# First feed-forward stage: norm weights applied where the transposes are emptied, a fixed order of the first conversions, constants loaded later

## The chip, the cores and the metric

One core of a Trainium2 chip runs the kernel in one launch. The metric is device time in microseconds, the median of several executions; the profile is one further execution, taken by the hardware profiler.

## What is computed

An encoder of two layers over 256 tokens of width 1024, in fp32. Each layer is a feed-forward block, an attention block (differential in the first layer, neighbourhood in the second) and a second feed-forward block, each with an RMS norm ahead of it and one behind:

```python
def _rmsnorm(x, g):
    y = xf * lax.rsqrt(jnp.mean(xf * xf, axis=-1, keepdims=True) + EPS)
    return (y * g.astype(jnp.float32)).astype(x.dtype)

def _swiglu(x, wg, wu, wd):
    return (jax.nn.silu(x @ wg) * (x @ wu)) @ wd

    h = h + FFN_RES * _rmsnorm(_swiglu(_rmsnorm(h, g[0]), ffn1_wg[i], ...), g[1])
```

The hidden width of the feed-forward blocks is 2816. The change is in the very first of them, up to the point where its pipeline is full.

## The kernel before

The 256 tokens are two tiles of 128 rows, `h[0]` and `h[1]`. Every matrix is kept as a sum of two fp32r parts, hi and lo, and a product is three: hi x hi, hi x lo, lo x hi. Weights come in pieces of 512 KB (128 x 1024 fp32). The class `Weights` plans them in one list. `load` issues a piece's DMA on SP's queue into one of four raw buffers; `split` makes hi on ScalarE (L130, a copy that rounds) and lo on VectorE (L131, raw minus hi), each in two halves of 512 columns, into one of nine part buffers. `get`, called where products need a piece, first splits that piece, then up to four ahead, then loads up to eight ahead. A raw buffer is free, and SP may issue the next DMA, when VectorE has made both lo halves.

The program is recorded in this order, and a scheduler sets the order on each engine by priorities (`high_priority` moves a block forward) and by `issue_after`, which puts instructions behind a given one on their engine. Every engine then runs its instructions in order, and waits are put in where data or buffers ask for them.

The first stage goes so. SP issues the two halves of `h[0]`, pieces 0 and 1 of `wg`, `h[1]`, pieces 2 and 3, two gain rows that are spread over 128 partitions (`gain`, L250), then the four pieces of `wu` (4 to 7), four column pieces (8 to 11) and so on. ScalarE issues one small DMA for the first gain row, and TensorE spreads it over the partitions with two matmuls against ones (L243) into two PSUM banks `g_first`. `first_norm` squares a tile on ScalarE (L282), takes the inverse root on POOL and multiplies by it and by the gain on VectorE (L307). `norm_T` transposes the two halves on TensorE, each into one PSUM bank (L365), and empties each bank with one 128x512 operation on ScalarE (hi, L355) and one on VectorE (lo, L356). POOL's queue loads `rope`, `mask` and `subg`, which are used in later stages.

`gu_rows` (through `proj_rows`, L380 to L383) makes four row products of 512 columns: g0 and g1 from `wg` for tiles 0 and 1, u0 and u1 from `wu`. Each has 24 matmuls: for each of eight blocks k of 128 rows hi x hi and hi x lo, and at the end lo x hi for all eight. `act` is the SiLU of g0 (L482), `gated` multiplies u0 by it on VectorE (L487) into `a`, which `to_T` transposes. From p = 2 on `gu_cols` makes products by columns (L414, L415): this is the column pass, and it uses the same pieces for both tiles. `down` (L438) adds products with `wd`.

Of the kernel before, what the change touches and what calls it, by code (L numbers as in the profile page):

```python
# [26 lines left out]
WARM = 1  # L27
# [49 lines left out]
class Weights:  # L77


    def __init__(self, tc, raw_pool, part_pool):  # L80
        self.tc = tc
        self.nc = tc.nc
        self.extras = []
        self.raw_pool = raw_pool
        self.part_pool = part_pool
        self.src = []
        self.key = {}
        self.raw = {}
        self.parts = {}
        self.n_dma = 0  # L90
        self.n_split = 0
        self.live = set()
        self.floor = 0

# [22 lines left out]
    def split(self, upto):  # L117
        nc = self.nc
        while self.n_split < min(upto, len(self.src)):
            i = self.n_split  # L120
            self.load(i + 1)
            ap = self.src[i]
            a, b = ap.shape[1], ap.shape[2]
            raw = self.raw.pop(i)
            hi = self.part_pool.tile([P, UE], F32R, tag="hi", name=f"whi{i}")
            lo = self.part_pool.tile([P, UE], F32R, tag="lo", name=f"wlo{i}")
            n = a * b
            for c in range(0, n, PIECE):
                e = slice(c, c + PIECE)
                nc.scalar.activation(hi[:, e], raw[:, e], AF.Copy)  # L130
                nc.vector.tensor_tensor(out=lo[:, e], in0=raw[:, e], in1=hi.bitcast(F32)[:, e], op=ALU.subtract)  # L131
            self.parts[i] = (
                hi[:, :n].rearrange("p (a b) -> p a b", b=b),
                lo[:, :n].rearrange("p (a b) -> p a b", b=b),
            )
            self.n_split += 1

    def get(self, key):
        i = self.key[key]
        self.split(i + 1)  # L140
        self.split(min(i + 1 + SPLIT_AHEAD, self.floor + PART_BUFS))
        self.load(min(i + 1 + DMA_AHEAD, self.n_split + RAW_BUFS))
        return self.parts[i]
# [8 lines left out]
def encoder_kernel(ctx, tc, x, norm_g, f1g, f1u, f1d, f2g, f2u, f2d,  # L152
# [79 lines left out]
    g_row = l4p.tile([1, D], F32, tag="l4", name="g_row")  # L232
    nc.scalar.dma_start(g_row, norm_g[0, 0:1, :])
    ones = t2p.tile([1, P], F32, tag="t2", name="ones")
    nc.vector.memset(ones, 1.0)
    warm = t2p.tile([P, NC], F32, tag="t2", name="warm")
    nc.vector.memset(warm, 0.0)
    for i in range(WARM):
        wps = ps_mm.tile([P, 512], F32, tag="mm", name=nm("warm_ps"))
        nc.tensor.matmul(wps, warm[:, :P], warm, start=True, stop=True)  # L240
# [7 lines left out]
    def gain(li, j, queue=nc.sync):  # L248
        t = gp.tile([P, D], F32, tag="gain", name=nm("gain"))
        queue.dma_start(t, bcast(norm_g[li, j, :], P))  # L250
        return t

# [4 lines left out]

    ident = const.tile([P, P], F32, name="ident")
# [3 lines left out]
    nc.vector.memset(mhalf, -0.5)  # L262
    rope = const.tile([P, NH, 2, 16], F32, name="rope")
    nc.gpsimd.dma_start(rope, ropec.rearrange("(t p) a b -> p t a b", p=P))
    mask = const.tile([P, GRID_W], F32, name="mask")
    nc.gpsimd.dma_start(mask, maskc)
    subg = const.tile([P, P], F32, name="subg")
    nc.gpsimd.dma_start(subg, bcast(dsub[0], P))
    bias = const.tile([P, 8, 6, GRID_W], F32, name="bias")

# [40 lines left out]
    def first_norm(t, gain_t):  # L311
        with tc.high_priority(offset=HP):
            return first_norm_(t, gain_t)

# [3 lines left out]

    def first_norm_(t, gain_t):
        ss = sm.tile([P, 2], F32, tag="ss2", name=nm("ss2"))  # L320
        for b, s in enumerate(HALVES):
            square(h[t][:, s], 1.0 / 32.0, ss[:, b:b + 1])
        return prenorm(t, gain_t, ss)
# [52 lines left out]
    def proj_rows(ps, xT, t, keys):  # L376
        parts = [W.get(key) for key in keys]
        w = [(wh[:, j, :], wl[:, j, :]) for wh, wl in parts for j in range(wh.shape[1])]
        for kt, (wh, wl) in enumerate(w):
            nc.tensor.matmul(ps, xT[0][:, t, kt, :], wh, start=kt == 0, stop=False)  # L380
            nc.tensor.matmul(ps, xT[0][:, t, kt, :], wl, start=False, stop=False)  # L381
        for kt, (wh, wl) in enumerate(w):
            nc.tensor.matmul(ps, xT[1][:, t, kt, :], wh, start=False, stop=kt == KT - 1)  # L383
# [87 lines left out]
    def ffn(key, li, gpre, xg1, xT, gpost, last, aside=None):  # L471
# [3 lines left out]
        def gu_rows(nme, t):  # L475
            ps = mm_tile()
            proj_rows(ps, xT, t, [(key, nme, 0, j) for j in range(KT * NC // UE)])
            return ps
# [41 lines left out]
        if key == "f10":  # L520
            s0 = act(gu_rows("g", 0))
            norm_T(xg1, xT, 1)
# [308 lines left out]
    xg0 = first_norm(0, g_first)  # L831
# [8 lines left out]
    xg1, xT = ffn("f10", 0, gain(0, 2), xg1, xT, gain(0, 1), False)  # L840
# [47 lines left out]
```

## Time and profile before

| | us |
|---|---|
| median of three runs | 1022.96 |
| lowest, highest | 1022.93, 1028.88 |
| profiled execution | 1023.75 |
| its span, first to last instruction | 1022.0 |

Times in the rows below are microseconds from the start of the span. A timeline row gives the start, the time until the last of its instructions ended, the engine, the line, what was written and read, how many instructions are taken together, and in brackets the engine's idle time before it and what ended that. PE is TensorE, ACT ScalarE, DVE VectorE. Matmuls overlap: their rate is read from start to start.

### The profile page before, as it was taken

The page shows a single profiled execution, that of the slowest core. Times are in us where ns is not written, and L with a number is a line of the kernel's source. Part 1 is how long each engine was busy: PE and PEld are TensorE (multiplying, and loading weights), DVE is VectorE, ACT ScalarE, POOL GpSimd, SP SyncE. Part 2 cuts the span into 40 slices and gives each one's busy share as a digit, 9 for nine tenths or more (in the row PEclk, how much of TensorE's full clock was granted, in tenths as well). Part 3 has the DMA queues.
Part 4 walks back from the last instruction along what each step waited for, and adds up shares of the span by engine and source line. Part 5 has one row for each costly group of instructions (what it writes and reads, how often), then busy time and mean ns, then how long its engine had stood idle before and what let it go on. Part 6 is the DMA issues. An engine that isn't in the chain of part 4 may idle for free.

```text
span 1022.0 us, 14666 instructions
## 1 busy us (share of the span) xinstructions
PE 1002.6 (98%) x5342; PEld 842.8 (82%) x5342; DVE 667.3 (65%) x1240; ACT 586.3 (57%) x1235; POOL 22.9 (2%) x38
## 2 busy tenths in 40 slices
PE   8999999999999999999999999999999999999997
PEld 5788888888777788888888888888898878888885
DVE  6766666577777666667577676657865477556572
ACT  6655556566776555656456555546765366555551
POOL 1000000000001000000000000000000010000000
PEclk9999999999999999999999999999999999999999
DMA  8866666375524666665377667646742446666631
GB/s 276 266 187 189 192 191 187 113 239 169 165 84 139 229 208 180 192 186 188 108 234 245 194 191 216 195 134 205 229 121 102 124 145 225 187 192 179 205 104 42
DMA packets 120825, 182.84 MB, mean 179 GB/s; under 512 B 5729, under 2 KB 87649, under 8 KB 120754
## 3 DMA queue, kind: packets, MB, share of 16 engines
q1 hardware_dynamic: 120608, 181.65, 57.3%
q8 instruction: 42, 0.69, 0.3%
q0 software_dynamic: 144, 0.26, 0.2%
q14 instruction: 29, 0.24, 0.1%
q10 hardware_dynamic: 2, 0.00, 0.0%
HBM read 180.84 MB, written 1.05 MB: 178 GB/s over the span
## 4 chain that ended last, share of the span: by engine, by line
PE 87%; DMA 4%; ACT 4%; DVE 3%; issue 1%; POOL 0%; SPq 0%; DVEq 0%; POOLq 0%; ACTq 0%
PE mm L414 25%; PE acc L438 24%; PE mm L415 13%; PE mm L380 5%; PE mm L381 5%; PE mm L383 5%; PE mm L438 2%; PE tr L365 2%; PE tr L702 2%; DMA raw<-in_ffn_wg_dram 2%; DVE wlo L131 2%; DMA raw<-in_ffn_wu_dram 1%; ACT whi L130 1%; DMA raw<-in_na_w_in_dram 1%; PE mm L397 1%
## 5 line engine op out<-in xcount | busy, mean ns | idle before, releaser
L131 DVE TENSOR_TENSOR wlo<-raw,whi 128x512 fp32r<-128x512 f32 x656 | 425.2, 686 | 178.5 <-ACT whi L130 170.8
L130 ACT ACTIVATE whi<-raw 128x512 fp32r<-128x512 f32 x656 | 379.2, 624 | 210.6 <-PE mm L414 52.8
L414 PE MATMUL mm<-xT,whi 128*128 128x512 f32 x1152 | 408.3, 399 | 0.8 <-DVE g L498 0.7
L415 PE MATMUL mm<-xT,wlo 128*128 128x256 f32 x1152 | 323.9, 281 | 0.0
L414 PEld LDWEIGHTS mm<-xT,whi 128*128 128x128 f32 x1152 | 216.7, 188 | 54.9 <-DVE g L498 1.7
L415 PEld LDWEIGHTS mm<-xT,wlo 128*128 128x128 f32 x1152 | 218.0, 189 | 1.1
L438 PE MATMUL acc<-whi,hT 128*128 128x512 f32 x704 | 197.3, 391 | 0.0
L438 PEld LDWEIGHTS acc<-whi,hT 128*128 128x128 f32 x704 | 130.3, 188 | 26.9
L380 PE MATMUL mm<-whi,xT 128*128 128x512 f32 x272 | 110.6, 407 | 2.9 <-ACT xT L355 2.8
L438 PE MATMUL acc<-wlo,hT 128*128 128x512 f32 x352 | 111.7, 391 | 0.0
L381 PE MATMUL mm<-wlo,xT 128*128 128x512 f32 x272 | 108.5, 399 | 0.0
L438 PEld LDWEIGHTS acc<-wlo,hT 128*128 128x128 f32 x352 | 66.1, 188 | 14.2
L383 PE MATMUL mm<-whi,xT 128*128 128x512 f32 x272 | 67.4, 390 | 0.0
L380 PEld LDWEIGHTS mm<-whi,xT 128*128 128x128 f32 x272 | 51.9, 191 | 16.4 <-ACT xT L355 5.2
L381 PEld LDWEIGHTS mm<-wlo,xT 128*128 128x128 f32 x272 | 51.9, 191 | 12.1 <-DVE wlo L131 2.0
L383 PEld LDWEIGHTS mm<-whi,xT 128*128 128x128 f32 x272 | 51.1, 188 | 10.5
L498 DVE TENSOR_TENSOR u<-mm,u 128x256 f32<-128x256 f32 x72 | 30.3, 421 | 32.1 <-ACT u L497 32.0
L497 ACT ACTIVATE g<-mm 128x256 f32<-128x256 f32 x72 | 26.9, 374 | 36.3 <-PE mm L415 36.3
L355 ACT ACTIVATE hT<-a 128x512 fp32r<-128x512 f32 x36 | 22.7, 630 | 41.1 <-DVE a L487 41.1
L498 DVE TENSOR_TENSOR g<-mm,g 128x256 f32<-128x256 f32 x72 | 30.2, 420 | 14.2 <-ACT g L497 14.2
L497 ACT ACTIVATE u<-mm 128x256 f32<-128x256 f32 x72 | 26.9, 374 | 17.0 <-PE mm L415 17.0
L356 DVE TENSOR_TENSOR hT<-a,hT 128x512 fp32r<-128x512 f32 x36 | 24.9, 693 | 17.3 <-ACT hT L355 16.1
(113 smaller groups left out, 811.0 us busy)
## 6 DMA issues: line engine op xcount, KB each, us to landing
raw<-in_ffn_wg_dram SPq DMA_DIRECT2D x88, 512.0 KB, 4.6
raw<-in_ffn_wu_dram SPq DMA_DIRECT2D x88, 512.0 KB, 4.5
raw<-in_ffn_wd_dram SPq DMA_DIRECT2D x88, 512.0 KB, 4.3
raw<-in_diff_w_in_dram SPq DMA_DIRECT2D x24, 512.0 KB, 4.8
raw<-in_na_w_in_dram SPq DMA_DIRECT2D x24, 512.0 KB, 4.8
gain<-in_norm_g_dram SPq DMA_DIRECT2D x11, 512.0 KB, 5.3
raw<-in_diff_w_out_dram SPq DMA_DIRECT2D x8, 512.0 KB, 3.9
raw<-in_na_w_out_dram SPq DMA_DIRECT2D x8, 512.0 KB, 4.6
```

The source lines that it names most:

```text
L130: nc.scalar.activation(hi[:, e], raw[:, e], AF.Copy)
L131: nc.vector.tensor_tensor(out=lo[:, e], in0=raw[:, e], in1=hi.bitcast(F32)[:, e], op=ALU.subtract)
L355: last_act[0] = nc.scalar.activation(hi, ps, AF.Copy)
L356: nc.vector.tensor_tensor(out=lo, in0=ps, in1=hi.bitcast(F32), op=ALU.subtract)
L380: nc.tensor.matmul(ps, xT[0][:, t, kt, :], wh, start=kt == 0, stop=False)
L381: nc.tensor.matmul(ps, xT[0][:, t, kt, :], wl, start=False, stop=False)
L383: nc.tensor.matmul(ps, xT[1][:, t, kt, :], wh, start=False, stop=kt == KT - 1)
L414: nc.tensor.matmul(ps, wh[:, j, c], xT.both(kt), start=kt == 0, stop=False)
L415: nc.tensor.matmul(ps[:, S:], wl[:, j, c], xT.one(0, kt), start=False, stop=kt == KT - 1)
L438: nc.tensor.matmul(ys[b], (xh, xl)[xp](i), parts[i][wp][:, 0, HALVES[b]], start=first and b not in seen, stop=last and left[b] == 0)
L497: nc.scalar.activation(y[:, f], ps[:, S:], AF.Copy)
L498: nc.vector.tensor_tensor(out=y[:, f], in0=ps[:, :S], in1=y[:, f], op=ALU.add)
```

## The change

Five things are changed, all in the first feed-forward stage.

1. The gain row is loaded as eight rows of 128 numbers, transposed by one small matmul and kept as eight columns `g_col`. `first_norm` only scales by the inverse root (a tensor_scalar); the gain is multiplied in when the transposes are emptied, which needs one operation per block of 128 columns, since each block has its own column of gains. `first_norm_T` replaces `norm_T` for the two tiles of this stage.
2. The first conversions and the evictions have a fixed order on ScalarE and VectorE: piece 0, four blocks, piece 1, four blocks. Conversions of pieces 2 and 3 and the second tile's norm follow. Tile 1's transposes and evictions are recorded behind the sixteenth matmul of g0 (`hooks`), and no piece beyond the fourth is split before them (`most`).
3. The warm-up is eleven bf16 matmuls of 128x128 by 512 columns instead of one in fp32.
4. The two spread gain rows, `rope`, `mask` and `subg` are loaded by SP at p = 3 of the column pass, behind the last weight DMA issued then.
5. The first DMAs are issued before the memsets and the identity are recorded; their order on SP is unchanged up to piece 3.

```diff
-    g_row = l4p.tile([1, D], F32, tag="l4", name="g_row")
-    nc.scalar.dma_start(g_row, norm_g[0, 0:1, :])
...
-    g_first = [bank(ps_acc, "acc") for _ in range(2)]
-    for s in range(2):
-        nc.tensor.matmul(g_first[s], ones, g_row[:, s * NC:(s + 1) * NC], start=True, stop=True)
...
+    g_rows = t2p.tile([KT, P], F32, tag="t2", name="g_rows")
+    nc.scalar.dma_start(g_rows, norm_g[0, 0, :].rearrange("(k p) -> k p", p=P))
...
+    def warm_up(n):
+
+        wb = warm.bitcast(BF16)
+        for i in range(n):
+            wps = ps_mm.tile([P, 512], F32, tag="mm", name=nm("warm_ps"))
+            nc.tensor.matmul(wps, wb[:, :P], wb[:, :NC], start=True, stop=True)
+
+    warm_up(WARM)
...
+    def load_constants():
+        nc.sync.dma_start(rope, ropec.rearrange("(t p) a b -> p t a b", p=P))
+        nc.sync.dma_start(mask, maskc)
+        nc.sync.dma_start(subg, bcast(dsub[0], P))
...
+                last_dve[0] = nc.vector.tensor_scalar(out=xn[-1], in0=h[t][:, s], scalar1=rs, scalar2=None,
+                                                      op0=ALU.mult)
...
+    def first_norm_T(xn, xT, t, between):
+
+        trs = [transposes(xn[b]) for b in range(2)]
+        for b in range(2):
+            last = between(b)
+            for j in range(4):
+                k = 4 * b + j
+                with behind(*last), tc.high_priority(offset=HP2):
+                    last = (nc.scalar.activation(xT[0][:, t, k, :], trs[b][:, j, :], AF.Copy, scale=g_col[:, k:k + 1]),
+                            nc.vector.scalar_tensor_tensor(
+                                out=xT[1][:, t, k, :], in0=trs[b][:, j, :], scalar=g_col[:, k:k + 1],
+                                in1=xT[0][:, t, k, :].bitcast(F32), op0=ALU.mult, op1=ALU.subtract))
+            last_act[0], last_dve[0] = last
...
-            s0 = act(gu_rows("g", 0))
-            norm_T(xg1, xT, 1)
+            s0 = act(gu_rows("g", 0, {2 * KT: lambda: first_norm_T(xg1, xT, 1, lambda b: ())}))
+            W.most = len(W.src)
+            with behind(last_act[0], last_dve[0]):
+                W.split(5)
...
+            if p == 3 and key == "f10":
+                with tc.issue_after(W.last_dma.ins):
+                    gpre, gpost = gpre(), gpost()
+                    load_constants()
...
-    norm_T(xg0, xT, 0)
-    with tc.issue_after(last_dve[0].ins):
-        W.split(2)
-    with tc.issue_after(last_act[0].ins):
+    def weights_first(b):
+        with behind(*((last_act[0], last_dve[0]) if b else (None, last_dve[0]))):
+            W.split(b + 1)
+        return W.last
+
+    first_norm_T(xg0, xT, 0, weights_first)
+    with behind(last_act[0], last_dve[0]):
+        xg1 = first_norm(1)
         W.split(4)
-        xg1 = first_norm(1, g_first)
```

ScalarE, from its first conversion on; `whi0` and `whi1` are the hi parts of pieces 0 and 1, the `tr` tiles the two PSUM banks of tile 0. Before:

```order
L130 ACTIVATE whi0_157<-raw0_107 128x512 [waits DMAHW3_49]
L130 ACTIVATE whi0_157<-raw0_107 128x512
L130 ACTIVATE whi1_163<-raw1_109 128x512 [waits DMAHW4_49]
L130 ACTIVATE whi1_163<-raw1_109 128x512
L355 ACTIVATE xT_9_142<-tr_10_143 128x4x128 [waits PE_49]
L355 ACTIVATE xT_9_142<-tr_11_150 128x4x128 [waits PE_49]
```

And now:

```order
L132 ACTIVATE whi0_168<-raw0_97 128x512 [waits DMAHW3_49]
L132 ACTIVATE whi0_168<-raw0_97 128x512
L399 ACTIVATE xT_18_157<-tr_19_158,g_col_155 128x128 [waits DVE_49,PE_49]
L399 ACTIVATE xT_18_157<-tr_19_158,g_col_155 128x128 [waits DVE_49] x3
L132 ACTIVATE whi1_182<-raw1_99 128x512 [waits DMAHW4_49]
L132 ACTIVATE whi1_182<-raw1_99 128x512
L399 ACTIVATE xT_18_157<-tr_20_163,g_col_155 128x128 [waits PE_49]
L399 ACTIVATE xT_18_157<-tr_20_163,g_col_155 128x128 [waits DVE_49] x3
```

The evictions moved between the conversions, and the three of a bank that follow its first wait for a semaphore of VectorE. The count that each waits for is the one that VectorE reaches with its own eviction (L400) of the block before; L400 waits for ScalarE's eviction of the same block.

ScalarE, at tile 1; `whi4` and `whi5` belong to `wu`, `s` is the SiLU of g0. Before:

```order
L355 ACTIVATE xT_9_142<-tr_27_269 128x4x128 [waits PE_49]
L130 ACTIVATE whi4_205<-raw4_203 128x512 [waits DMAHW2_49]
L355 ACTIVATE xT_9_142<-tr_28_276 128x4x128 [waits PE_49]
L130 ACTIVATE whi4_205<-raw4_203 128x512
L130 ACTIVATE whi5_219<-raw5_211 128x512 [waits DMAHW3_49]
```

And now:

```order
L399 ACTIVATE xT_18_157<-tr_33_250,g_col_155 128x128 [waits PE_49]
L399 ACTIVATE xT_18_157<-tr_34_255,g_col_155 128x128 [waits PE_49]
L399 ACTIVATE xT_18_157<-tr_33_250,g_col_155 128x128 [waits DVE_49]
L399 ACTIVATE xT_18_157<-tr_34_255,g_col_155 128x128 [waits DVE_49]
L399 ACTIVATE xT_18_157<-tr_33_250,g_col_155 128x128 [waits DVE_49]
L399 ACTIVATE xT_18_157<-tr_34_255,g_col_155 128x128 [waits DVE_49]
L521 ACT_TABLE_LOAD
L521 ACTIVATE s_35_284<-mm_32_225 128x512 [waits PE_49]
L399 ACTIVATE xT_18_157<-tr_33_250,g_col_155 128x128 [waits DVE_49]
L399 ACTIVATE xT_18_157<-tr_34_255,g_col_155 128x128 [waits DVE_49]
L132 ACTIVATE whi4_286<-raw4_226 128x512 [waits DMAHW0_49]
```

The first conversion of `wu` stood between the two evictions of tile 1, and now stands behind all eight and behind the table load and the SiLU. Two of the eight stand behind the SiLU.

VectorE, where u0 is gated into `a`; `wlo8` to `wlo11` are the lo parts of the first four column pieces. Before:

```order
L131 TENSOR_TENSOR wlo11_336<-raw11_241,whi11_335 128x512 x2
L487 TENSOR_TENSOR a_32_367<-mm_31_310,s_26_267 128x512
L131 TENSOR_TENSOR wlo12_407<-raw12_317,whi12_406 128x512 x2
L356 TENSOR_TENSOR hT0_24_201<-tr_33_369,hT0_23_200 128x4x128
L131 TENSOR_TENSOR wlo13_423<-raw13_325,whi13_422 128x512 x2
```

And now:

```order
L133 TENSOR_TENSOR wlo8_347<-raw8_293,whi8_346 128x512 x2
L133 TENSOR_TENSOR wlo9_355<-raw9_301,whi9_354 128x512 x2
L133 TENSOR_TENSOR wlo10_363<-raw10_309,whi10_362 128x512 x2
L526 TENSOR_TENSOR a_39_402<-mm_38_345,s_35_284 128x512
L133 TENSOR_TENSOR wlo11_371<-raw11_317,whi11_370 128x512 x2
L133 TENSOR_TENSOR wlo12_442<-raw12_352,whi12_441 128x512
```

The gating stood behind the differences of piece 11, and now stands behind those of piece 10.

## Rows read from the trace of the kernel before

**Rows 1.** The page: busy time, and the clock in 40 slices.
```profile
PE 1002.6 (98%) x5342; PEld 842.8 (82%) x5342; DVE 667.3 (65%) x1240; ACT 586.3 (57%) x1235; POOL 22.9 (2%) x38
...
PEclk9999999999999999999999999999999999999999
```

**Rows 2.** Waits of TensorE, 0 to 40.05 us: total, times, longest.
```profile
PE tr L365 <- DVE a L487: 2.0, 1, 2.0
...
PE mm L380 <- ACT xT L355: 1.4, 1, 1.4
```

**Rows 3.** Waits of TensorE, 40 to 1022 us, the first entry.
```profile
PE mm L380 <- ACT xT L355: 1.4, 5, 0.3
```

**Rows 4.** Timeline of TensorE: start us, us, what, count, idle before.
```profile
10.74 0.80 PE L380 MATMUL mm<-whi,xT 128*128 128x512 f32 x1 [1.42 <-ACT xT L355]
...
12.19 0.63 PE L381 MATMUL mm<-wlo,xT 128*128 128x512 f32 x1
12.61 0.63 PE L380 MATMUL mm<-whi,xT 128*128 128x512 f32 x1
...
24.64 1.98 PE L383 MATMUL mm<-whi,xT 128*128 128x512 f32 x8
...
40.05 0.39 PE L414 MATMUL mm<-xT,whi 128*128 128x512 f32 x1
```

**Rows 5.** The chain of waits, 0 to 50 us: start us, us, what.
```profile
1.65 6.06 DMA raw<-in_ffn_wg_dram
...
9.72 9.19 DMA raw<-in_ffn_wu_dram
...
22.71 1.28 ACT L482
...
26.47 5.81 DMA raw<-in_ffn_wu_dram
...
34.93 0.04 issue
34.98 0.66 PE tr L365 x4
```

**Rows 6.** Timeline of ScalarE, 0 to 75 us.
```profile
7.74 1.15 ACT L130 ACTIVATE whi<-raw 128x512 fp32r<-128x512 f32 x2 [2.82 <-DMA raw<-in_ffn_wg_dram]
...
10.11 1.06 ACT L355 ACTIVATE xT<-tr 128x512 fp32r<-128x512 f32 x2
...
14.89 1.65 ACT L130 ACTIVATE whi<-raw 128x512 fp32r<-128x512 f32 x3
...
29.83 1.15 ACT L130 ACTIVATE whi<-raw 128x512 fp32r<-128x512 f32 x2 [0.65 <-DMA raw<-in_ffn_wu_dram]
...
74.13 0.63 ACT L130 ACTIVATE whi<-raw 128x512 fp32r<-128x512 f32 x1 [0.25 <-ACT whi L130]
```

**Rows 7.** Timeline of VectorE, 0 to 45 us.
```profile
7.41 0.75 DVE L307 SCALAR_TENSOR_TENSOR xg<-h,pre,acc 128x512 f32<-128x512 f32 x1 [0.86 <-PE acc L243]
...
10.72 0.69 DVE L356 TENSOR_TENSOR xT<-tr,xT 128x512 fp32r<-128x512 f32 x1 [1.02 <-ACT xT L355]
```

**Rows 8.** Groups by line and shape: count, busy us, mean ns, idle before.
```profile
L282 ACT ACTIVATE junk<-tr,rz 128x128 bf16<-128x128 f32 x16 | 5.9, 371 | 4.7 <-PE tr L702 4.3
...
L728 DVE SCALAR_TENSOR_TENSOR o<-tr,sub,subg 128x128 f32<-128x128 f32 x16 | 4.6, 344 | 0.0
...
L307 DVE SCALAR_TENSOR_TENSOR xg<-h,pre,acc 128x512 f32<-128x512 f32 x4 | 2.9, 744 | 1.5 <-PE acc L243 0.9 <-POOL pre L297 0.7
```

**Rows 9.** The page: DMA issues, KB each, median us to landing.
```profile
raw<-in_ffn_wg_dram SPq DMA_DIRECT2D x88, 512.0 KB, 4.6
```

**Rows 10.** Timeline of SP's queue, 0 to 70 us.
```profile
4.58 1.84 SPq L250 DMA_DIRECT2D gain<-in_norm_g_dram  x2
...
24.41 2.43 SPq L106 DMA_DIRECT2D raw<-in_ffn_wu_dram  x2
...
65.70 3.74 SPq L106 DMA_DIRECT2D raw<-in_ffn_wg_dram  x2
```

More of the change, by code (lines that the diff above doesn't have):

```diff
@@ L1 @@
 import math
-from contextlib import ExitStack
+from contextlib import ExitStack, contextmanager
 import concourse.bass as bass
@@ L93, in __init__ @@
         self.floor = 0
+        self.most = 4
     def add(self, key, ap):
@@ L129, in split @@
                 e = slice(c, c + PIECE)
[L130 to L131 removed]
+                self.last = (
+                    nc.scalar.activation(hi[:, e], raw[:, e], AF.Copy),
+                    nc.vector.tensor_tensor(out=lo[:, e], in0=raw[:, e], in1=hi.bitcast(F32)[:, e], op=ALU.subtract))
             self.parts[i] = (
@@ L256, in encoder_kernel @@
     W.load(4)
+    warm = t2p.tile([P, NC], F32, tag="t2", name="warm")
+    nc.vector.memset(warm, 1.0)
     ident = const.tile([P, P], F32, name="ident")
@@ L374, in norm_T, with first_norm, behind, proj_rows @@
             transpose_split(xg[b], xT[0][:, t, k, :], xT[1][:, t, k, :])
-    def proj_rows(ps, xT, t, keys):
+    def first_norm(t):
+        with tc.high_priority(offset=HP):
+            ss = sm.tile([P, 2], F32, tag="ss2", name=nm("ss2"))
+            for b, s in enumerate(HALVES):
+                square(h[t][:, s], 1.0 / 32.0, ss[:, b:b + 1])
+            rs = rsqrt2(ss, EPS, "pre")
+            xn = []
+            for b, s in enumerate(HALVES):
+                xn.append(t2p.tile([P, NC], F32, tag="t2", name=nm("xn")))
+                last_dve[0] = nc.vector.tensor_scalar(out=xn[-1], in0=h[t][:, s], scalar1=rs, scalar2=None,
+                                                      op0=ALU.mult)
+            return xn
+    @contextmanager
+    def behind(*last):
+        with ExitStack() as st:
+            for i in last:
+                if i is not None:
+                    st.enter_context(tc.issue_after(i.ins))
+            yield
+    def first_norm_T(xn, xT, t, between):
[10 more added lines that the diff above has]
+            last_act[0], last_dve[0] = last
+    def proj_rows(ps, xT, t, keys, hooks={}):
+        count = [0]
+        def product(*a, **k):
+            m = nc.tensor.matmul(*a, **k)
+            count[0] += 1
+            if count[0] in hooks:
+                with tc.issue_after(m.ins):
+                    hooks[count[0]]()
         parts = [W.get(key) for key in keys]
@@ L379, in proj_rows @@
         for kt, (wh, wl) in enumerate(w):
-            nc.tensor.matmul(ps, xT[0][:, t, kt, :], wh, start=kt == 0, stop=False)
-            nc.tensor.matmul(ps, xT[0][:, t, kt, :], wl, start=False, stop=False)
+            product(ps, xT[0][:, t, kt, :], wh, start=kt == 0, stop=False)
+            product(ps, xT[0][:, t, kt, :], wl, start=False, stop=False)
         for kt, (wh, wl) in enumerate(w):
-            nc.tensor.matmul(ps, xT[1][:, t, kt, :], wh, start=False, stop=kt == KT - 1)
+            product(ps, xT[1][:, t, kt, :], wh, start=False, stop=kt == KT - 1)
         if t == NH - 1:
@@ L473, in ffn, with gu_rows @@
         hT = {}
-        def gu_rows(nme, t):
+        def gu_rows(nme, t, hooks={}):
             ps = mm_tile()
-            proj_rows(ps, xT, t, [(key, nme, 0, j) for j in range(KT * NC // UE)])
+            proj_rows(ps, xT, t, [(key, nme, 0, j) for j in range(KT * NC // UE)], hooks)
             return ps
@@ L829, in attn @@
         return xg, nxT
-    xg0 = first_norm(0, g_first)
-    xT = xt_tiles("xT")
-    norm_T(xg0, xT, 0)
-    with tc.issue_after(last_dve[0].ins):
-        W.split(2)
-    with tc.issue_after(last_act[0].ins):
+    xg0 = first_norm(0)
+    g_tr = bank(ps_tr, "tr")
+    nc.tensor.transpose(g_tr[:, :KT], g_rows, ident[:KT, :KT])
+    g_col = sm.tile([P, KT], F32, tag="g_col", name="g_col", bufs=1)
+    nc.vector.tensor_copy(g_col, g_tr[:, :KT])
+    xT = xt_tiles("xT")
+    def weights_first(b):
[5 more added lines that the diff above has]
+        xg1 = first_norm(1)
         W.split(4)
-        xg1 = first_norm(1, g_first)
-    xg1, xT = ffn("f10", 0, gain(0, 2), xg1, xT, gain(0, 1), False)
+    xg1, xT = ffn("f10", 0, lambda: gain(0, 2), xg1, xT, lambda: gain(0, 1), False)
     xg1, xT = attn("a0", 0, gain(0, 4), xg1, xT, gain(0, 3))
```

30 lines of the change are left out of this document (6 added, 24 removed).

## Prediction

> **What bounds the kernel now.** I read the page first. TensorE is busy for 1002.6 us, 98% of the span [rows 1], so the time can only move where TensorE waits or runs at its lower rate. Its waits come next: between 0 and 40 us there are 2.0 us for the gated tile `a` and 1.4 us for the first eviction [rows 2]; from there to the end the longest entry is 1.4 us, in five pieces [rows 3]. The first product of the column pass starts at 40.05 us [rows 4], and from then on TensorE is fed. So the change is worth what it moves that start by, one for one, unless its loads in the middle of the stage make a new wait.
>
> TensorE's rate changes in the first 40 us. Matmuls of 512 columns start 0.43 us apart at 12 us, and eight of them take 1.98 us at 24 us, which is some 0.225 us from start to start [rows 4]: 512 columns in 0.43 us is 1.2 GHz, the later spacing is the 2.4 GHz level. The page's clock row reads nine tenths or more all along [rows 1], so here the level is read from the spacing. Ahead of the slow stretch TensorE had been idle for 1.42 us [rows 4].
>
> The chain that leads to 40.05 us is hardly TensorE's at all [rows 5]: 6.06 us for the first `wg` piece, 9.19 us for the first `wu` piece, conversions, a table load of 1.28 us, 5.81 us for the fourth column piece, the gating of `a`, its transposes. Transfers and the two converting engines bound the first stage.
>
> **The change part by part.** *Head.* The two fp32 matmuls that spread the gain row go; VectorE's second `xg` waited for them until 7.41 us [rows 7]. The gains now come in as eight columns. Eleven bf16 matmuls of 512 columns run instead, which at 0.43 us each are 4.7 us from about 1.5 us, over at 6.2 us, when the first normalized half is about ready; loads and norm hide them. They should bring the 2.4 GHz level before the products.
>
> *First piece of weights.* It lands at 7.71 us (1.65 + 6.06 [rows 5]), and ScalarE starts on it at 7.74 us [rows 6]. Nothing ahead of it on SP changes, but what shares the DMA engines does: two 512 KB gain copies and three small copies from POOL go to later. One end is 7.71 us, nothing gained; the other is 1.65 plus the median of 4.6 us that such a piece takes in the whole run [rows 9], 6.25 us. I take 7.2 us, nearer to the row of this very transfer.
>
> *Evictions of tile 0.* Before: two of 128x512 in 1.06 us on ScalarE, after four conversions [rows 6]. After, by the order rows: two conversions, four evictions of 128x128, two conversions, four evictions. The first product can start sooner: 7.2 + 1.15 for two conversions, 0.37 for one short eviction, makes 8.7 us against 10.74 us. But each further eviction in a bank waits for VectorE, and the count it waits for is reached by VectorE's eviction of the block before, which waits for ScalarE's in its turn. The two engines pass the bank to and fro. A ScalarE operation on 128x128 out of PSUM with a scale per partition takes 0.371 us, a VectorE one 0.344 us [rows 8]; for a hand-over I take 0.03 us, after the 0.04 us of the chain [rows 5]. A block costs 0.371 + 0.344 + 0.06 = 0.775 us, four cost 3.1 us, where a whole bank took ScalarE 0.53 us. Behind the last block stand, in ScalarE's queue, the second tile's squares and the conversions of pieces 2 and 3.
>
> Step by step: block 0 is done on ScalarE at 8.7, block 1 at 9.8 (VectorE first makes the two differences of piece 0, 0.69 us each), blocks 2 and 3 at 10.6 and 11.4. Piece 1 is converted to 12.4; block 4 follows, block 5 waits again, and block 7 is done at 15.4. Two squares and four conversions end at 18.9 us; before, the last three of these ended at 16.54 us (14.89 + 1.65 [rows 6]). VectorE then scales the second tile and makes the last three differences, done at 21.1 us.
>
> The scaling is a tensor_scalar, which the trace lacks. The nearest row is the fused scaling of the same tile, 0.744 us with two tensors read [rows 8]; one tensor read may cost the same, or half. I take 0.6 us; the half would lower the sum by 0.5 us, the whole raise it by 0.3, with two on the path. In a sentence apart: the Trainium skill's "VectorE: DVE Perf Modes" (Mode 2×_2P) says that an fp32 tensor_scalar from SBUF to SBUF uses both read ports and passes two elements a cycle; no row here shows one, and by it (an estimate) the two would take the half, and the sum would be 0.5 us less.
>
> *Tile 1.* The sixteenth product of g0 ends at 21.4 us, the transposes 0.8 us later, the last eight products at 24.0. Tile 1's evictions alternate between two banks: three rounds of 0.775 us to 24.35, then the table load of 1.28 us, the SiLU of 0.6, and only then blocks 3 and 7 (26.4 and 26.7 us). TensorE can do three pairs of g1, to 25.35, and waits 1.1 us for block 3. The other 18 products end at 30.5 us, where u0 starts; before, the products of g1 ended at 26.6 us (24.64 + 1.98 [rows 4]).
>
> *Pieces of wu.* Their eight conversions, 0.53 us apart, stand behind block 7: from 26.6 on, the last difference at 32.2 us, just ahead of u0, which runs 24 x 0.225 = 5.4 us to 35.9. That the first of them now lands sooner is worth nothing, since ScalarE can't take it. Column pieces are issued as differences free a buffer: the third at 30.8 us instead of 24.41 [rows 10]. Before, its conversion waited for its landing until 29.83 us [rows 6], 5.4 us after issue; so it lands at 36.2. Two conversions and two differences make 38.1, and the gating of `a`, which now stands behind the third piece instead of the fourth, ends at 38.7 us. TensorE has done six products of u1 by 37.3 and waits 1.4 us, where it waited 2.0. Four transposes (some 0.6) and 18 products (4.05) end at 43.45.
>
> So the column pass starts at 43.45 instead of 40.05 us, 3.4 us later. The profiled execution took 1023.75 us and would take 1027.15; the median shown, 1022.96 us, is 0.8 us lower, so 1026.3 us.
>
> By the Trainium skill's "PSUM — Partial Sum Buffer" (PSUM bank collisions raise a hardware error) no two engines may touch one bank at once, reads against reads included, so two engines can't empty one bank side by side. The trace agrees as far as it goes: VectorE took the first bank at 10.72 us, when ScalarE had moved to the second [rows 6, 7]. By this rule the to and fro stays; without it the sum would be that of the first rival.
>
> *Loads in the middle.* Two gain copies (0.92 us of issue each [rows 10]) and three small ones now stand on SP between column pieces, near 65 us. The piece behind was issued at 65.70 us [rows 10]; with the median of 4.6 us [rows 9] it landed at 70.3, and it was converted at 74.13 us [rows 6]. That leaves 3.8 us, in which some 2.5 us of issue and a part of 1.2 MB of transfers fit. I price it at nothing; without that cover at one more such landing, 4.6 us.
>
> **The rivals.** *The transfers bind, not the evictions.* If blocks overlap and the to and fro costs nothing, the same chain gives the last conversion at 15.4, g0's sixteenth product at 17.9 and the column pass at 39.6 us; and at 38.6 if pieces 2 and 3 land a microsecond sooner. That is 0.45 to 1.45 us less than before, 1021.5 to 1022.5, say 1022.0. For it: the chain of before is mostly transfers [rows 5], and 1 MB goes out of its way. Against: the order rows name the waits. It decides if a block costs under 0.3 us.
>
> *The rate falls back.* From 8.7 to 21.4 us TensorE does 16 products of 0.225 us, 3.6 us in 12.7. If it is at 1.2 GHz again at 21.4, transposes and first products take double: g0 ends at 27.3, g1 at 32.7, the column pass starts at 45.4, 5.35 us later: 1028.3 us. For it: after the break before 10.74 us the products of before ran at the lower level [rows 4]. Against: after the wait of 2.0 us for `a` they went on at the upper one, 20 products and the transposes in 5.1 us between 34.98 and 40.05 [rows 4, 5].
>
> *The mid-stage loads show.* They add up to 4.6 us to the forecast: 1030.9. Against it stands the spare time, for it that SP is one queue.
>
> **How the numbers follow.** Forecast 0.55, transfers bind 0.18, the rate falls back 0.21, loads show 0.06. The forecast's own range comes from the first landing and the scaling together: a start of the column pass between 42.0 and 44.2 us, so 1024.9 to 1027.1. For 8 in 10 the range must reach into both neighbours: down to 1021.8, which takes most of the fast rival, and up to 1028.8, past the rate's. One per cent is 10.2 us, about what a measurement of this kernel can tell from no change; no case comes near it. Faster by more would need the column pass before 30 us, and 96 products of 0.225 us after a start at 8.7 end at 30.3 without a single wait. Faster 0.01, within 0.97, slower 0.02.
>
> **What would show it right or wrong.** Right: evictions of tile 0 on ScalarE about 0.8 us apart, each with idle time that VectorE ends; the first product near 8.7 us; the last of g0's pairs near 21; a wait of about 1 us before g1's fourth block; the first column product near 43.5 us; no new wait of TensorE near 75 us. Wrong: evictions 0.3 us apart; 0.43 us between products after 21 us; a conversion near 75 us that waits for a transfer.

## The result, and the profile after

The changed kernel takes 1030.47 us, the median of seven runs (1028.86 to 1034.14), where the kernel before took 1022.97 us in seven runs beside them: a ratio of 1.0068, 95% interval 1.0051 to 1.0084. It is slower by 7.5 us, where 3.4 were forecast. The measured time lies above the range, whose top was 1028.8 us. The profiled execution took 1031.11 us, its span 1028.7 us.

TensorE does the same work in a longer span. The page of the changed kernel, to be held against [rows 1]:

```profile
PE 1002.9 (97%) x5348; PEld 842.4 (82%) x5348; DVE 669.2 (65%) x1252; ACT 589.5 (57%) x1247; POOL 21.0 (2%) x35
...
PEclk7999999999999999999999999999999999999999
```

Its busy time is the same to 0.3 us, and only the first slice of the clock row differs. The timeline of TensorE, which answers to [rows 4], says where the time went:

```profile
9.87 0.50 PE L410 MATMUL mm<-whi,xT 128*128 128x512 f32 x1 [2.28 <-ACT xT L399]
...
17.86 0.80 PE L410 MATMUL mm<-whi,xT 128*128 128x512 f32 x1 [2.31 <-ACT whi L132]
...
22.27 0.63 PE L410 MATMUL mm<-whi,xT 128*128 128x512 f32 x1
22.69 0.63 PE L410 MATMUL mm<-wlo,xT 128*128 128x512 f32 x1
23.12 1.91 PE L358 MATMUL tr<-ident,xn 128*128 128x128 f32 x8
24.68 2.50 PE L410 MATMUL mm<-whi,xT 128*128 128x512 f32 x9
...
42.12 0.66 PE L358 MATMUL tr<-ident,a 128*128 128x128 f32 x4 [1.73 <-DVE a L526]
...
46.74 0.39 PE L453 MATMUL mm<-xT,whi 128*128 128x512 f32 x1
```

The column pass starts at 46.74 us instead of 40.05, 6.69 us later. From there to the span's end it is 1028.7 - 46.74 = 981.96 us, and it was 1022.0 - 40.05 = 981.95 us. So what the span lost lies in the first stage. That the two agree to 0.01 us is in part chance: in the profiled executions of the runs below this rest takes 980.9 to 985.1 us. Outside the span the execution lost another 0.66 us: 1031.11 - 1028.7 = 2.41 us, where it was 1023.75 - 1022.0 = 1.75 us. The waits of TensorE behind the start of the column pass begin with the same entry as in [rows 3]:

```profile
PE mm L410 <- ACT xT L348: 1.4, 5, 0.3
```

ScalarE's timeline, against [rows 6]:

```profile
8.41 1.15 ACT L132 ACTIVATE whi<-raw 128x512 fp32r<-128x512 f32 x2 [3.36 <-DMA raw<-in_ffn_wg_dram]
9.47 0.35 ACT L399 ACTIVATE xT<-tr,g_col 128x128 fp32r<-128x128 f32 x1
10.67 0.37 ACT L399 ACTIVATE xT<-tr,g_col 128x128 fp32r<-128x128 f32 x1 [0.85 <-DVE xT L400]
11.45 0.37 ACT L399 ACTIVATE xT<-tr,g_col 128x128 fp32r<-128x128 f32 x1 [0.42 <-DVE xT L400]
12.24 0.37 ACT L399 ACTIVATE xT<-tr,g_col 128x128 fp32r<-128x128 f32 x1 [0.42 <-DVE xT L400]
...
18.32 1.66 ACT L132 ACTIVATE whi<-raw 128x512 fp32r<-128x512 f32 x3
```

Its evictions stand 0.79 us apart, each behind 0.42 us of idle time that VectorE's eviction of the block before ends. VectorE's timeline has the counterpart, and the new scaling:

```profile
11.07 0.35 DVE L400 SCALAR_TENSOR_TENSOR xT<-tr,g_col,xT 128x128 fp32r<-128x128 f32 x1 [0.43 <-ACT xT L399]
...
19.28 0.88 DVE L379 TENSOR_SCALAR xn<-h,pre 128x512 f32<-128x512 f32 x2 [0.67 <-POOL pre L300]
```

The to and fro is there as forecast. What the forecast didn't have is the level of TensorE's rate. In the windows of the changed kernel the column behind POOL is the granted clock:

```profile
10.00:12.00 2.00, 1.52 (x4) 0.46 (x4) 1.13 (x4) 0.73 (x2) 0.00 (x0) 0.86 0.83 284
12.00:14.00 2.00, 0.83 (x3) 0.39 (x2) 1.40 (x4) 1.66 (x4) 0.00 (x0) 0.50 0.78 278
22.00:24.00 2.00, 2.00 (x9) 1.60 (x8) 0.00 (x0) 0.00 (x0) 0.00 (x0) 0.50 0.82 274
24.00:26.00 2.00, 2.00 (x10) 1.83 (x9) 0.89 (x3) 1.14 (x4) 0.00 (x0) 0.72 0.67 226
26.00:28.00 2.00, 2.00 (x11) 1.57 (x9) 1.04 (x4) 1.83 (x4) 0.00 (x0) 1.00 0.03 11
```

It is half, the 1.2 GHz level, from 12 to past 24 us. Before it fell, TensorE had waited 2.28 us, made two products, waited 0.48 us and made two more. The products at 22.27 and 22.69 us stand 0.42 us apart, though their operands are there.

The first landing differs between executions, so two starts of the column pass can't be compared as they are. In the ten profiled executions without early gain copies (the changed kernel and nine of the runs below) ScalarE's first conversion starts at 5.85 us in one, at 6.88 to 7.71 in eight, and at 8.41 in the changed kernel's. Below, "the distance" is from the start of that conversion to the column pass: 40.05 - 7.74 = 32.31 us before, 46.74 - 8.41 = 38.33 us after, 6.0 us more.

### The profile page after: what moved, and what is told of

Its sections match the earlier page's. It is cut to its first block, busy times and chain, and to the rows that moved or that the text cites. A ratio compares the mean times of both kernels' runs of the same rounds, so it can differ in the third digit from the quotient of the medians.

```text
span 1028.7 us, 14699 instructions
## 1 busy us (share of the span) xinstructions
PE 1002.9 (97%) x5348; PEld 842.4 (82%) x5348; DVE 669.2 (65%) x1252; ACT 589.5 (57%) x1247; POOL 21.0 (2%) x35
## 4 chain that ended last, share of the span: by engine, by line
PE 88%; ACT 4%; DVE 4%; DMA 3%; issue 1%; POOL 1%; SPq 0%; DVEq 0%; POOLq 0%; ACTq 0%
PE mm L453 26%; PE acc L477 24%; PE mm L410 15%; PE mm L454 13%; PE tr L358 2%; PE mm L477 2%; PE tr L747 2%; DVE wlo L133 2%; DMA raw<-in_ffn_wg_dram 1%; ACT whi L132 1%; DMA raw<-in_na_w_in_dram 1%; PE mm L436 1%; PE mm L437 1%; PE mm L438 1%; ACT junk L285 1%
## 5 line engine op out<-in xcount | busy, mean ns | idle before, releaser
L537 DVE TENSOR_TENSOR g<-mm,g 128x256 f32<-128x256 f32 x72 | 30.3, 421 | 13.9 <-ACT g L536 13.8
L323 DVE TENSOR_TENSOR yg<-acc,gain 128x512 f32<-128x512 f32 x20 | 13.7, 687 | 32.5 <-ACT junk L285 32.3
L285 ACT ACTIVATE junk<-acc 128x512 bf16<-128x512 f32 x20 | 11.8, 590 | 38.3 <-PE acc L477 38.3
```

Of the source, the lines that this page charges most:

```text
L285: nc.scalar.activation(junk[:, :n], src, AF.Square, scale=scale, accum_out=acc)
L537: nc.vector.tensor_tensor(out=y[:, f], in0=ps[:, :S], in1=y[:, f], op=ALU.add)
```

## The experiments

Theory A: the block-wise emptying, a bank handed to and fro, is the cause, and starves TensorE. Rivals: the rate of TensorE alone, the fixed order of the conversions, the loads in the middle of the stage. Each run is compared with the kernel before on the same chip. In the runs' sources the lines are shifted by a few. No runs were made under the numbers e7 and e8.

| run | edit | ratio to before | interval | distance, us |
|---|---|---|---|---|
| (changed kernel) | | 1.0068 | 1.0051 to 1.0084 | 38.33 |
| e1 | part 1 undone | 0.9999 | 0.9983 to 1.0015 | 31.31 |
| e2 | neighbouring blocks in two banks | 1.0035 | 1.0018 to 1.0051 | 35.09 |
| e3 | TensorE kept busy | 1.0038 | 1.0024 to 1.0052 | 36.64 |
| e4 | wu conversions free | 1.0055 | 1.0031 to 1.0079 | 37.65 |
| e5 | a bank's four blocks on ScalarE first | 1.0017 | 0.9999 to 1.0034 | 34.47 |
| e6 | e5, wu free, u0 gated early | 0.9987 | 0.9971 to 1.0002 | 29.78 |
| e9 | early constants | 1.0082 | 1.0062 to 1.0102 | 40.31 |
| e10 | before, u0 gated early | 0.9990 | 0.9977 to 1.0003 | 29.36 |
| e11 | e1, wu free, u0 gated early | 0.9974 | 0.9960 to 0.9988 | 29.00 |
| e12 | one warm-up matmul | 1.0049 | 1.0032 to 1.0065 | 37.54 |
| e13 | e11, one warm-up matmul | 0.9976 | 0.9965 to 0.9986 | 29.57 |

### e1: whole banks

```diff
-                    last = (nc.scalar.activation(xT[0][:, t, k, :], trs[b][:, j, :], AF.Copy, scale=g_col[:, k:k + 1]), ...)
+                last = (nc.scalar.activation(xT[0][:, t, k, :], trs[b], AF.Copy),
+                        nc.vector.tensor_tensor(out=xT[1][:, t, k, :], in0=trs[b], ...))
```

with `g_first` and its two fp32 matmuls back in the norm.

> Part 1 of the change is undone and all else is kept: the gain row is spread by two fp32 matmuls and multiplied in the norm, and each PSUM bank is emptied by one 128x512 operation per engine. If the block-wise emptying is the cause (ScalarE and VectorE handing one bank to and fro, 0.79 us a block, eight blocks), the last conversion of the first four pieces ends near 16.5 us instead of 19.98, tile 1 loses some 2 us less, and the column pass starts near 41.5 us: 1025.5 us, at most 1 us above or below. If the fixed order of the conversions or the loads in the middle of the stage are the cause, it stays within 1 us of the changed kernel's 1030.5. If the slower rate of TensorE alone is the cause and does not come from starved products, it also stays at 1030.

The ratio is 0.9999: the loss is gone. The timeline of ScalarE, one operation per bank, and of the last conversions:

```profile
8.99 0.60 ACT L397 ACTIVATE xT<-tr 128x512 fp32r<-128x512 f32 x1
9.49 1.14 ACT L132 ACTIVATE whi<-raw 128x512 fp32r<-128x512 f32 x2
...
12.78 1.66 ACT L132 ACTIVATE whi<-raw 128x512 fp32r<-128x512 f32 x3
```

The last conversion ends at 14.44 us, 6.7 us behind the first one's start instead of 11.6; more than expected, since the pieces had landed by then. The distance falls by 7.0 us. Part 1 carries the loss; with the other parts kept, the kernel is as fast as before. The run doesn't say whether the number of operations or the to and fro costs, nor what the rate adds.

### e2: neighbouring blocks in two banks

```diff
+            trs = [bank(ps_tr, "tr").rearrange("p (j q) -> p j q", q=P) for _ in range(2)]
+            for k in range(KT):
+                nc.tensor.transpose(trs[k % 2][:, k // 2, :], xn[k // 4][:, (k % 4) * P:(k % 4 + 1) * P], ident)
```

for tile 0 only.

> Blocks with gain columns as in the changed kernel, but tile 0's even blocks are transposed into one PSUM bank and its odd blocks into the other, so that neighbouring blocks never share a bank. If the sharing of a bank is what couples the two engines, ScalarE's second eviction follows its first at 0.37 us instead of 1.2, the evictions of blocks 4 to 7 take some 1.6 us instead of 3.1, the last conversion ends near 17.7 us instead of 19.98, and the column pass starts near 44.4 us: 1028.2 us. If the number of operations is what costs, not the sharing, ScalarE's evictions stay 0.8 us apart and the time stays at 1030.5.

ScalarE's timeline:

```profile
8.52 0.61 ACT L406 ACTIVATE xT<-tr,g_col 128x128 fp32r<-128x128 f32 x2
9.72 0.63 ACT L406 ACTIVATE xT<-tr,g_col 128x128 fp32r<-128x128 f32 x2 [0.59 <-DVE xT L407]
```

Two blocks of different banks follow each other without a gap, and only the third waits for VectorE. Four blocks take 1.83 us instead of 3.14 (9.47 to 12.61 in the changed kernel). The distance falls by 3.2 us, the ratio to 1.0035, a little more than expected; the interval ends at 1.0051, where the changed kernel's begins. The sharing couples the engines. It is the bank and not the tile `xT`: VectorE reads ScalarE's `xT` here too, and the second eviction follows all the same.

### e5: the same operations in another order

```diff
-                    last = (nc.scalar.activation(...),
-                            nc.vector.scalar_tensor_tensor(...))
+                    hi = nc.scalar.activation(...)
+                last = (hi,) + tuple(last[1:])
+            for j in range(4):
+                k = 4 * b + j
+                with behind(*last), tc.high_priority(offset=HP2):
+                    lo = nc.vector.scalar_tensor_tensor(...)
+                last = (hi, lo)
```

> The changed kernel with the same 32 block operations, in another order: ScalarE empties all four blocks of a bank, then VectorE takes the four. If handing the bank to and fro is the cause, ScalarE's four evictions take about 1.2 us instead of 3.1, twice over, the last conversion of the first four pieces ends some 4 us sooner after the first, tile 1's eight take 2.1 us instead of 3.9, and the column pass starts about 33.5 us behind the first conversion instead of 38.3: near 1025.7 us, a ratio to the kernel before of 1.002. If the larger number of operations is the cause, it stays within 1.5 us of the changed kernel: a ratio of 1.0055 to 1.0068.

The ratio is 1.0017, as theory A expected, and outside what the number of operations would give. ScalarE's timeline has the four evictions in one row of 1.12 us:

```profile
8.53 1.12 ACT L399 ACTIVATE xT<-tr,g_col 128x128 fp32r<-128x128 f32 x4
```

The distance is 34.47 us, 1 us more than expected. TensorE's timeline shows where it is:

```profile
35.82 1.12 PE L358 MATMUL tr<-ident,a 128*128 128x128 f32 x4 [2.64 <-DVE a L531]
36.59 0.78 PE L415 MATMUL mm<-whi,xT 128*128 128x512 f32 x1
37.16 0.63 PE L415 MATMUL mm<-wlo,xT 128*128 128x512 f32 x1
37.59 0.63 PE L415 MATMUL mm<-whi,xT 128*128 128x512 f32 x1
```

After a wait of 2.64 us for the gated tile, the next products stand 0.43 us apart: the rate had fallen.

### e3: TensorE kept busy

```diff
+            with behind(last_pe[0]):
+                dummies(10)
+            s0 = act(gu_rows("g", 0, {2: lambda: dummies(3), 4: lambda: dummies(6), 8: lambda: dummies(13),
+                                      11: lambda: dummies(6), ...
```

`dummies(n)` is n bf16 matmuls of 128x128 by 512 columns into a bank of `accs`.

> The changed kernel with 38 extra bf16 matmuls of 512 columns, put on TensorE where it waits between its first products (10 ahead of the first, then 3, 6, 13 and 6), into a bank that is written anew later. They add nothing to the result. If the lower rate is a part of the loss by itself, TensorE stays at its upper level: products near 22 us stand 0.23 us apart instead of 0.43, tile 1's transposes take 1.3 us instead of 1.9, g0 ends near 25.0 us instead of 27.0 and the column pass starts 2.0 us sooner: 1028.5 us. If the rate costs nothing because ScalarE sets the pace, the time stays within 0.5 us of 1030.5; if the extra matmuls stand in the way of products, it is up to 2 us more.

The granted clock stays at 1.00, here in one of the windows that read 0.50 after the change:

```profile
12.00:14.00 2.00, 1.89 (x8) 0.79 (x6) 1.72 (x4) 1.15 (x4) 0.00 (x0) 1.00 0.38 147
```

Tile 1's transposes take 1.03 us, from 21.54 us on:

```profile
21.54 1.03 PE L359 MATMUL tr<-ident,xn 128*128 128x128 f32 x8
...
22.33 2.30 PE L411 MATMUL mm<-whi,xT 128*128 128x512 f32 x9
...
44.22 0.39 PE L454 MATMUL mm<-xT,whi 128*128 128x512 f32 x1
```

The ratio falls to 1.0038, with an interval that just touches the changed kernel's, and the distance by 1.7 us where 2.0 were expected. ScalarE's evictions are still 0.79 us apart. So the rate is a part of the loss by itself, and the smaller one: e5, where the to and fro is gone, got 3.9 us of distance back.

### e4: pieces of wu free

```diff
+            W.most = 8
             s0 = act(gu_rows("g", 0, ...
             W.most = len(W.src)
-            with behind(last_act[0], last_dve[0]):
-                W.split(5)
```

> The changed kernel without the hold on the pieces of wu: all four may be converted ahead of tile 1's evictions, and the order that put piece 4 behind them is gone. If the fixed order is a main cause, raw buffers come free some 8 us sooner, the column pieces are issued near 22 us instead of 31.3, the wait of 1.7 us for the gated tile goes, and the column pass starts 3 to 4 us sooner: 1027 us. If the block-wise emptying is the cause, the conversions only push tile 1's evictions back by their own time, and it stays within 1 us of 1030.5, or above it.

The ratio, 1.0055, can't be told from the changed kernel's, and the distance is 0.7 us shorter. SP issues the first column piece at 21.21 us instead of 31.30, and the wait for the gated tile shrinks from 1.73 to 1.12 us, but conversions now stand between tile 1's evictions. The distance makes e4 look worse than it is: its first piece landed so early (5.85 us) that the first eviction had to wait 0.66 us for TensorE's transposes, and stands 1.81 us behind the first conversion instead of 1.06. Without these 0.75 us it would be some 1.4 us shorter, still far from the 3 to 4 us that the order as a main cause would have given. The order is no main cause.

### e9: constants early

```diff
+    nc.gpsimd.dma_start(rope, ...)
+    nc.gpsimd.dma_start(mask, maskc)
+    nc.gpsimd.dma_start(subg, bcast(dsub[0], P))
...
-                    gpre, gpost = gpre(), gpost()
-                    load_constants()
...
+    xg1, xT = ffn("f10", 0, gain(0, 2), xg1, xT, gain(0, 1), False)
```

> Part 4 of the change is undone and all else kept: the two gain rows stand on SP's queue behind the first pieces again, the three small copies on POOL's. If the loads in the middle of the stage cost something, the time falls by up to 4.6 us, a ratio of 1.002 to the kernel before. If the early copies are what kept the first pieces late before, the first pieces now land later and the ratio rises above 1.0075. If the block-wise emptying is the whole loss, neither shows: the ratio stays within 0.001 of 1.0068.

The ratio is 1.0082, on the side of the second theory, with an interval that overlaps the changed kernel's. But that theory's mechanism isn't there: the first conversion starts at 7.45 us, as early as in most runs without the copies. The profiled execution, the slowest of its six, took 1034.74 us. Its column pass starts 1.02 us later than in the changed kernel, though the first conversion was 0.96 us earlier. What it lost of this stage stands behind a wait of 2.06 us for the gated tile, in TensorE's timeline:

```profile
41.53 0.66 PE L357 MATMUL tr<-ident,a 128*128 128x128 f32 x4 [2.06 <-DVE a L525]
...
42.33 0.63 PE L409 MATMUL mm<-wlo,xT 128*128 128x512 f32 x1
42.76 0.63 PE L409 MATMUL mm<-whi,xT 128*128 128x512 f32 x1
...
47.76 0.39 PE L452 MATMUL mm<-xT,whi 128*128 128x512 f32 x1
```

From the transposes to the column pass it is 6.23 us, and 46.74 - 42.12 = 4.62 in the changed kernel: the products run at the lower rate again. A larger part was lost far behind: from the column pass to the end of the span it is 1032.9 - 47.76 = 985.14 us instead of 981.96, and between 740 and 750 us, where TensorE waited 1.5 us for ScalarE instead of 0.7, the granted clock reads 0.83 instead of 1.00. Nothing in the record ties these later losses to the edit. Whether the time of e9 differs from the changed kernel's stays open; undoing the late loads shows no gain, and 4.6 us are excluded. SP's timeline of the changed kernel shows the late loads between two pieces:

```profile
71.57 0.90 SPq L271 DMA_DIRECT2D gain<-in_norm_g_dram  x2
...
74.18 1.94 SPq L107 DMA_DIRECT2D raw<-in_ffn_wg_dram  x2
```

### e12 and e13: one warm-up matmul

```diff
-WARM = 11
+WARM = 1
```

> Part 3 of the change undone in number: one warm-up matmul in bf16 instead of eleven, all else as in the changed kernel. If the eleven keep TensorE at its upper level for the products that count, the column pass starts later without them: up to 1 us, a ratio of 1.0078. If the first products wait for ScalarE whatever their rate, and the level falls in the waits anyway, nothing changes: a ratio within 0.001 of 1.0068.

> The fastest run (whole banks, wu pieces free, u0 gated early) with one warm-up matmul instead of eleven. If the warm-up brings the upper level sooner to products that count, its loss shows: products from 9 to 16 us stand 0.43 us apart as in the kernel before, the column pass starts some 30 us behind the first conversion instead of 29.0, and the ratio to the kernel before is 0.9985. If the differences of the fourth wg piece set the pace of g0 anyway, it stays within 0.001 of 0.9974.

e12 came out at 1.0049, beside the 0.001 given and on the side that no theory had; its interval overlaps that of 1.0068, so a loss by the warm-up stays open. e13 and e11 agree (0.9976 and 0.9974). The eleven matmuls bring no gain in either kernel.

### e6, e10 and e11: what holds the column pass back then

After e5 TensorE waits 2.64 us for the gated tile, which stands behind the differences of late column pieces, as it did before [rows 2, 5]. Two edits go at that: no hold on `wu` (as in e4), and

```diff
+            W.most = 10
+            u0 = gu_rows("u", 0)
+            a0 = gated(u0, s0)
+            W.most = len(W.src)
+            with tc.issue_after(last_a[0].ins):
+                W.split(12)
```

> The run with all four blocks of a bank on ScalarE first, and two edits more: the pieces of wu may be converted ahead of tile 1's evictions, and VectorE gates u0 ahead of the differences of the third and fourth column pieces. If what is left then is the gated tile behind late column pieces, TensorE's wait for it (1.7 us) goes, the column pass starts near 31 us behind the first conversion, and the ratio to the kernel before is 0.998, some 2 us under it. If the column pass then waits for its own pieces, the wait only moves and the ratio is 1.001 to 1.002.

> The kernel before with one edit: VectorE gates u0 ahead of the differences of the third and fourth column pieces. If TensorE's wait of 2.0 us for the gated tile is the only thing that holds the column pass back, its first product starts some 2 us sooner and the ratio is 0.998. If the column pass then waits for its pieces, the ratio is 1.000.

> The run with whole banks (part 1 undone) and the two edits that helped the run with ScalarE first: pieces of wu may be converted ahead of tile 1's evictions, and VectorE gates u0 ahead of the third and fourth column pieces. If the emptying and the wait for the gated tile are all that holds the column pass back, it starts some 29 us behind the first conversion, as with blocks on ScalarE first (29.8) or a little sooner, and the ratio to the kernel before is 0.998, from 0.9965 to 0.9995. If ScalarE's wait for a third piece of wu, which now stands ahead of tile 1's evictions, decides, the start falls back to 31 us and the ratio is 1.000.

The wait is gone in all three. TensorE's timeline of e11 (its first four rows are used in the last section):

```profile
5.56 1.98 PE L264 MATMUL acc<-g_row,ones 1*128 1x512 f32 x4
7.60 1.90 PE L364 MATMUL tr<-ident,xg 128*128 128x128 f32 x8
...
9.81 0.63 PE L408 MATMUL mm<-wlo,xT 128*128 128x512 f32 x1
10.24 0.63 PE L408 MATMUL mm<-whi,xT 128*128 128x512 f32 x1
...
31.46 0.66 PE L364 MATMUL tr<-ident,a 128*128 128x128 f32 x4
...
36.53 0.39 PE L451 MATMUL mm<-xT,whi 128*128 128x512 f32 x1
```

Its column pass starts 29.0 us behind the first conversion, not 31, so ScalarE's wait of 1.45 us for a third piece of `wu`, ahead of tile 1's evictions, doesn't decide. e11 came out at 0.9974: it beats the kernel before by 0.26% and the changed one by 1 - 0.9974 / 1.0068 = 0.93%. It is the changed kernel without part 1 and with the two edits. e6 and e10 lie between 1.000 and 0.998 with intervals that reach past 1. For e6 that excludes the 1.001 to 1.002 of the second theory, and the distance of 29.78 us is even shorter than the 31 of the first; for e10 the time doesn't decide between the two. In e10 the distance fell by 2.95 us and the time by about 1. In the profiled execution 2.7 us are given back behind the start (1021.5 - 36.87 = 984.63 us from there to the end, 981.95 before), some of it in waits of TensorE in the column pass. The kernel before, then e10:

```profile
PE mm L414 <- DVE g L498: 0.7, 1, 0.7
```

```profile
PE mm L416 <- DVE g L500: 1.9, 3, 1.1
```

## Why the prediction was wrong

The direction and the mechanism were right, the size wasn't: two steps were mis-sized, and they add up. Forecast and measured, from the span's start:

| step | forecast, us | measured, us |
|---|---|---|
| first conversion starts | 7.2 | 8.41 |
| one block | 0.775 | 0.79 |
| last conversion ends, behind the first one's start | 11.7 | 19.98 - 8.41 = 11.57 |
| last difference ends, likewise | 13.9 | 21.97 - 8.41 = 13.56 |
| from there to the column pass | 22.35 | 46.74 - 21.97 = 24.77 |

**The evictions** went as worked out, to 0.4 us over thirteen; e2 and e5 show that it is the to and fro that costs. Two ways around it are shown: neighbours in different banks, or all of one engine's reads first. The Trainium skill's "PSUM — Partial Sum Buffer" (PSUM bank collisions raise a hardware error) keeps two engines out of one bank. These kernels always wait there, and no run lets two engines into one bank.

**The rate** is the step that failed first. The forecast ran g0's end, tile 1's transposes and g1 at the upper level and gave the lower one a rival's chance of 0.21, at 1.95 us more. It fell, from 12 to past 24 us; e3 took that away and got 1.7 us of distance back. The forecast's distance was 43.45 - 7.2 = 36.25 us, and e3's, where the rate is as forecast, is 36.64. The lower rate works through tile 1: its transposes end late, so its evictions, the conversions of `wu` and the issue of the column pieces come late too. The third column piece, on SP's queue of the changed kernel:

```profile
33.71 1.57 SPq L107 DMA_DIRECT2D raw<-in_ffn_wu_dram  x2
```

It is issued 33.71 - 8.41 = 25.3 us behind the first conversion, where 30.8 - 7.2 = 23.6 was forecast; in e3 it is 31.27 - 7.58 = 23.7. Its conversion starts 5.8 us later where 5.4 was taken.

The argument against that rival was one row: after the wait of 2.0 us for `a` the products before went on at the upper level [rows 4]. That row doesn't carry so far. After 2.64 us in e5 and 2.06 us in e9 the level had fallen, and in the changed kernel it fell behind 2.28 us and 0.48 us of waiting with two products between. The length of one wait doesn't settle it either: after 2.22 us, in TensorE's timeline of e1, the products go on at the upper level, and the column pass follows 39.01 - 33.94 = 5.07 us behind, as in the kernel before.

```profile
33.94 0.66 PE L363 MATMUL tr<-ident,a 128*128 128x128 f32 x4 [2.22 <-DVE a L523]
```

That the rival's price comes so near is partly luck. It had g0 end at 27.3 us, where its own terms, transposes of 1.6 us and eight products of 0.43 us from 21.4, give 26.4; and in the changed kernel the level rose again between 24 and 26 us, so that g0 ended by 27.0 though the first piece had landed 1.2 us later.

**The first landing**, taken at 7.2 us because 1.2 MB go out of the way, is the other. It came at 8.41 us in the profiled execution. Over the runs, early copies make no difference that shows: 7.45, 7.51 and 7.74 us in the three kernels with them, 7.47 to 7.71 in seven of ten without. The row of the same transfer, 7.71 us [rows 5], was the better value, and the spread from 5.85 to 8.41 us belonged in the range.

So 46.74 is 43.45 + 1.21 for the landing + 2.08 behind it, most of which is the rate. With the rate's rival as the likeliest case and the landing of [rows 5], the sum would have been 1028.8 us or so, still 1.7 under the median. In the profiled execution the rest is 0.70 us by which the first piece came later than 7.71, 0.13 us by which the 2.08 exceed the rival's 1.95, and 0.66 us outside the span. This last part shows in every run: the time outside the span is 1.71 to 1.86 us in the kernel before and e10, 2.07 to 2.41 us in the changed kernel and all runs that keep part 4, and 1.76 to 2.07 us in e9, which undoes it. So part 4 goes with some 0.35 us (a median of 2.26 us in the changed kernel, 1.9 in e9) that the sum didn't have; why, no run shows.

**The other steps.** Loads in the middle show no cost within the span, as forecast (e9). One sign that the prediction had named for the contrary is there in small: at 81.20 us a conversion of a `wg` piece waits 0.63 us for its transfer; TensorE waits for nothing between 66 and 100 us. The wait for the gated tile shrank to 1.73 us as expected (1.4). The scaling took 0.88 us for two of 128x512 where 1.2 was taken. The Trainium skill's "VectorE: DVE Perf Modes" (Mode 2×_2P) says that such an operation passes two elements a cycle. The trace agrees roughly: 0.44 us each, where half of the 0.744 us of the fused form [rows 8] is 0.37. The rival by which transfers bind is what e1 does without the to and fro: a distance 1.0 us under that of before, in the 0.45 to 1.45 us that were worked out, though its time is the same as before within 1.6 us. The prediction also took one per cent for about the least that a measurement of this kernel can tell; the interval of the result, 1.0051 to 1.0084, lies clear of no change.

## What to carry to other kernels

Before splitting one PSUM eviction into several to fold a scale in, see which engine reads the bank next: where two engines alternate on it, as here, each block costs both durations and two hand-overs (0.79 us of 0.37, 0.35 and 0.07), and recording all reads of one engine first, or spreading neighbours over two banks, takes most of that away. Where a change puts waits between single matmuls, price the rest of that stretch at TensorE's lower rate too, and don't dismiss that case by one wait of the same length: here the level held behind 2.22 us in one run and fell behind 2.06 us in another. Compare starts relative to the first landing, since that alone moved by up to 2.6 us between executions, and check that a very early landing can be used at all (e4).

## What had not been expected of the hardware

The clock column doesn't tell the whole rate. In the kernel before, and in e12, which have one short warm-up, it reads 1.00 while products stand 0.43 us apart ([rows 4] and the second fence below); after eleven warm-up matmuls the same spacing goes with 0.50. The window of e12, and two products of it:

```profile
12.00:14.00 2.00, 1.53 (x3) 0.99 (x4) 1.83 (x4) 1.20 (x3) 0.00 (x0) 1.00 0.62 227
```

```profile
13.79 0.63 PE L410 MATMUL mm<-whi,xT 128*128 128x512 f32 x1
14.22 0.63 PE L410 MATMUL mm<-wlo,xT 128*128 128x512 f32 x1
```

And a busy TensorE isn't always at its upper level. In e11 it runs eleven bf16 matmuls, the fp32 spreading of the gain row and the transposes from 1.59 to 9.5 us almost without a gap, and its first products, the rows at 9.81 and 10.24 us above, still stand 0.43 us apart. Here the clock column shows it, in the window from 8 to 10 us:

```profile
8.00:10.00 2.00, 1.93 (x9) 1.41 (x8) 2.00 (x4) 2.00 (x5) 0.00 (x0) 0.52 1.00 382
```

Why the level fell there is open.
